# Attention: the high part of V's differences made on GpSimd, and scores emitted in parts of up to 512 keys

## The chip, the core and the metric

The kernel runs on one core of a Trainium2 chip. A core has TensorE (PE, matrix products; PEld is its loading of weights), VectorE (DVE), ScalarE (ACT) and GpSimd (POOL); SyncE (SP) issues the DMAs. Each engine works through its own instructions in order, and an instruction that waits holds up everything behind it on that engine. The metric is the device time of one execution in microseconds (us).

## The reference, cut to what matters

Two layers on a stream of 1024 positions of 1024 features: a Mamba-2 layer, then a layer of stick-breaking attention with 16 heads of 64 features. Between and after them stands a gated per-layer embedding. The change is in the attention:

```
for blk in range(s // SB_BLOCK):                       # 8 blocks of 128 queries
    z = einsum('bhtd,bhsd->bhts', q[:, :, q0:kend], k[:, :, :kend])
    log_keep = where(strict, log_sigmoid(-z), 0.0)
    suffix = cumsum(log_keep, reverse) - log_keep
    weights = where(strict, exp(log_sigmoid(z) + suffix), 0.0)
    outs.append(einsum('bhts,bhsd->bhtd', weights, v[:, :, :kend]))
```

With keep = sigmoid(-z), the product P of the keeps after a key is a running product, and a weight is a difference of two neighbouring P. So the kernel computes the running product P alone and multiplies it by the differences of neighbouring rows of V, which gives the same sum.

## The kernel before, in words

Matrix products of full precision are made from three products of two parts: a high part in the format that TensorE multiplies fast (`F32R`), and a low part, the value less its high part. The positions are stored in reverse, so that the keys of a query block come after it.

The attention takes two heads at a time, in 8 pairs (`hp`), and for each pair four steps p = 3, 2, 1, 0 of two query blocks: 32 steps, and two more to drain. Three things go on at once in `step(i)`:

- for step i itself, the projections of its two blocks (`project`, 24 products of 128x384 each, in four portions of six) and, for p = 3 and 2, half of the gate (`gate`, 24 products of 128x512). These are the filling: nothing in the same step needs them;
- for step i-1, `flip` (four transposes of the normalised k and q on TensorE, L879, then ACT and DVE write the high and low parts `kst`, `qh`, `ql`) and `scores` of two heads times two blocks: the products z (L901, L902), the sigmoid on ACT into `pt` (L903), and one running product (scan) on DVE along all keys of the block (L904);
- for step i-2, `turn` (transposes of `pt` on TensorE into `tr`, L916 and L919, the high part `wh` on ACT, L925, the low part `wl` on DVE, L926) and `product` with V (L936).

TensorE's order is written out by hand: a `manual_schedule` covers that engine alone. The pieces of steps i-1 and i-2 have positions between 0 and 1 (`SPREAD`, `FLIP`), and a piece comes when so much of the filling has been emitted. For p = 1 and 0 the filling counts 10 and its portions only add up to 8; for p = 3 and 2 it counts 17, and they add up to 14. The pieces with a position beyond 0.8 therefore stand at the end of a step with no filling between them. The order on ACT, DVE, POOL and SP is set by the scheduler.

At the end of step i, `values` makes the differences of V's rows: DMAs on SP copy `vr` one row on into `vs` (L847 is the large one), POOL subtracts (L853), ACT writes the high part into `V` (L858), and POOL writes the low part (L859). `vs` has one buffer; `V` has six, and its first reader is the product two steps later. `norm` then normalises k and q on DVE (L867 to L870). The PSUM tiles `tr` and `z` have two buffers each. The weights of the next pair are loaded and split into `g0h` (ACT, L104) and `g0l` (DVE, L108) along the way.

Of the kernel before, what the change touches and what calls it, by code (L numbers as in the profile page):

```python
# [8 lines left out]
F32 = mybir.dt.float32  # L9
# [4 lines left out]
ALU = mybir.AluOpType  # L14
# [4 lines left out]
P = 128  # L19
S = 1024  # L20
# [13 lines left out]
NEX = 5  # L34
EARLY = 3
LASTP = ((0, 0, 512), (1, 0, 256), (1, 256, 256))
SPREAD = ((0.05, 0.95), (0.7, 1.0))
FLIP = 0.55
FILL = {32: (7, (4, 5, 6, 7)), 33: (6, ())}
CHUNKS = {30: (0, 1, 2, 3)}  # L40

# [742 lines left out]
def attention(k, A, rawp, hT, oTd, dbg, b2, pairs):  # L784


    tc, nc = k.tc, k.nc
# [3 lines left out]
    with ExitStack() as ctx:  # L791
        pp = ctx.enter_context(tc.tile_pool(name="b_pair", bufs=1, reuse_waits="tile"))
        wk = ctx.enter_context(tc.tile_pool(name="b_work", bufs=2, reuse_waits="tile"))
# [6 lines left out]
        keep = pp.tile([P, S], BF16, name="keep")  # L800
# [7 lines left out]
        def begin_pair(st):  # L808
            st["V"], st["vr"], st["v0"] = {}, {}, {}
            st["GT"] = pairs.gt.tile([P, S], F32, name="GT")  # L810

        def project(st, b):
            W = st["W"]
            ps = mm.tile([P, 512], F32, name="mm")
            prs = []
            sl = slice(b % 4 * P, b % 4 * P + P)
            for kk in range(KT):
                whi, wlo = W[kk]
                prs += terms((hh[b // 4][:, kk, sl], hl[b // 4][:, kk, sl]), (whi[:, :384], wlo[:, :384]))
            yield from split3_some(nc, ps[:, :384], prs, 6)  # L820
            p = b // 2
            if b % 2:
                st["kq"] = wk.tile([P, 2, 2, P], F32, name="kq", bufs=2)
                st["vr"][p] = wk.tile([P, 2, P], F32, name="vr", bufs=3)
            nc.scalar.copy(st["kq"][:, b % 2], ps.rearrange("p (m c) -> p m c", c=256)[:, :, 0:128])
            nc.vector.tensor_copy(st["vr"][p][:, b % 2], ps[:, 128:256])  # L826
            yield

        def gate(st, half):
            W = st["W"]  # L830
            gp = mm.tile([P, 512], F32, name="mm")
            sl = slice(half * 512, half * 512 + 512)
            prs = []
            for kk in range(KT):
                whi, wlo = W[kk]
                prs += terms((whi[:, 384:], wlo[:, 384:]), (hh[half][:, kk], hl[half][:, kk]))
            yield from split3_some(nc, gp, prs, 4)
            sg = wk.tile([P, 512], F32, name="sg", bufs=1)
            nc.scalar.activation(sg, gp, AF.Sigmoid)
            nc.vector.tensor_tensor(st["GT"][:, sl], gp, sg, op=ALU.mult)  # L840
            yield

        def values(st, p):

            vr = st["vr"][p]
            vs = wk.tile([P, 2, P], F32, name="vs", bufs=1)
            nc.sync.dma_start(vs[0:P - 1], vr[1:P])  # L847
            nc.sync.dma_start(vs[P - 1:P, 0], vr[0:1, 1])
            nc.sync.dma_start(vs[P - 1:P, 1], st["vr"][p + 1][0:1, 0] if p < 3 else zrow)
            st["v0"][p] = sm.tile([P, 2], F32, name="v0", bufs=4)  # L850
            for i in range(2):
                nc.sync.dma_start(st["v0"][p][:, i:i + 1], vr[0:1, i])
            nc.gpsimd.tensor_tensor(vs, vs, vr, op=ALU.subtract)  # L853
            V = st["V"][p] = wk.tile([P, 2, 256], F32R, name="V", bufs=6)
            Vx = V.rearrange("p b (x c) -> p b x c", c=64)
            d = vs.rearrange("p b (h c) -> p b h c", c=64)
            for i in range(2):
                nc.scalar.copy(Vx[:, i, 0::3], d[:, i])  # L858
                nc.gpsimd.tensor_tensor(Vx[:, i, 1:3], d[:, i], Vx[:, i, 0::3].bitcast(F32), op=ALU.subtract)  # L859

        def norm(st, p):
# [11 lines left out]
        def flip(st, p):  # L873
            kn = st.pop(("kn", p))
            tsl = slice(p * 256, (p + 1) * 256)
            tq = trp.tile([P, 512], F32, name="tr")
            for i in range(2):
                for m in range(2):
                    nc.tensor.transpose(tq[:, m * 256 + i * P:m * 256 + (i + 1) * P], kn[:, i, m], ident)  # L879
            kt, qt = tq[:, 0:256], tq[:, 256:512]  # L880
            qh = wk.tile([P, 2, 256], F32R, name="qh", bufs=1)
            for h in range(2):
                o, x = own[h], own[1 - h]
                g = k.gkq[o]
                nc.scalar.activation(kst[o, h, tsl], kt[o], AF.Copy, scale=g)
                nc.vector.scalar_tensor_tensor(  # L886
                    kst[x, h, tsl], kt[o], g, kst[o, h, tsl].bitcast(F32), op0=ALU.mult, op1=ALU.subtract)
                nc.scalar.copy(qh[o, h], qt[o])
                nc.scalar.copy(qh[x, h], qt[o])
                nc.vector.tensor_tensor(ql[o, h], qt[o], qh[o, h].bitcast(F32), op=ALU.subtract)  # L890
            st["q", p] = qh

        def scores(st, h, b):
            qh = st["q", b // 2]
            N = (NT - b) * P
            qs = slice((b % 2) * P, (b % 2) * P + P)
            pt = wk.tile([P, S], F32, name="pt", bufs=5)
            for ko, n in ([(0, N)] if N <= 512 else [(0, N // 2), (N // 2, N // 2)]):
                z = zp.tile([P, 512], F32, name="z")
                rk = kst[:, h, b * P + ko:b * P + ko + n]  # L900
                nc.tensor.matmul(z[:, :n], lhsT=qh[:, h, qs], rhs=rk, start=True, stop=False)  # L901
                nc.tensor.matmul(z[:, :n], lhsT=ql[:, h, qs], rhs=rk, start=False, stop=True)  # L902
                nc.scalar.activation(pt[:, ko:ko + n], z[:, :n], AF.Sigmoid, scale=-1.0)  # L903
            nc.vector.tensor_tensor_scan(pt[:, :N], pt[:, :N], keep[:, :N], 1.0, op0=ALU.mult, op1=ALU.max)  # L904
            st["a", h, b] = pt

        def turn(st, p, h, j0):

# [57 lines left out]
        n = len(steps)  # L966

        def spread(fns, a, z):
            m = len(fns)
            return [(a + (z - a) * (i + 0.5) / m, f) for i, f in enumerate(fns)]  # L970

        def combine_pieces(st, p):

            units = [(h, j) for h in range(2) for j in range(2 * p, NT, 2)]
            def prod(h, j):
                product(st, p, h, j)
                if j == NT - 2:
                    fold(st, p, h)
            fns = []
            for i, (h, j) in enumerate(units):  # L980
                fns.append(lambda h=h, j=j: turn(st, p, h, j))
                if i >= 2:
                    fns.append(lambda u=units[i - 2]: prod(*u))
            return fns + [lambda u=u: prod(*u) for u in units[-2:]]

        def step(i):
            pieces = []
            if i >= 2:
                hp, p = steps[i - 2]
                pieces += spread(combine_pieces(sts[hp], p), *SPREAD[0])  # L990
            if 1 <= i <= n:
                hp, p = steps[i - 1]
                st = sts[hp]
                pieces.append((FLIP, lambda st=st, p=p: flip(st, p)))
                units = [(lambda st=st, h=h, b=b: scores(st, h, b)) for h in range(2) for b in (2 * p + 1, 2 * p)]
                pieces += spread(units, *SPREAD[1])
            pieces.sort(key=lambda x: x[0])
            fill = []
            if i < n:
                hp, p = steps[i]  # L1000
                if p == NT // 2 - 1:
                    pairs.all(hp)
                    begin_pair(sts[hp])
                    if hp + 1 < 8:
                        pairs.start(hp + 1)
                    else:
                        b2.begin(pairs)
                fill = [(project(sts[hp], 2 * p + 1), 5)]
                if p >= 2:
                    fill.append((gate(sts[hp], p - 2), 7))  # L1010
                fill.append((project(sts[hp], 2 * p), 5))
            total = sum(w for _, w in fill)
            done = 0
            for f, w in fill:
                for _ in f:
                    done += 1
                    while pieces and pieces[0][0] <= done / total:
                        pieces.pop(0)[1]()
            if i < n:
                if p in LOADS:  # L1020
                    pairs.step(hp + 1)
                values(sts[hp], p)
                norm(sts[hp], p)
                if i in CHUNKS:
                    b2.weights(CHUNKS[i])
            for _, f in pieces:
                f()
# [226 lines left out]
```

## Time and profile before

| what | value |
|---|---|
| median of 3 runs | 1968.86 us (1968.41 to 1986.42) |
| the profiled execution | 1967.15 us, of which the span is 1965.4 us |
| PE busy | 1757.7 us (89%) |
| DVE busy | 1174.0 us (60%) |
| ACT busy | 901.1 us (46%) |
| POOL busy | 377.3 us (19%) |
| chain that ended last | PE 59%, DMA 15%, DVE 15%, ACT 7% |
| the DMA from `vr` to `vs` in that chain | 13% |

The span runs from the first to the last instruction, and the rest of the execution's time lies around it. The chain that ended last is followed back from the last instruction, at each step to what released it. The attention takes from about 943 to about 1780 us of the span.

### The profile page before, as it was taken

Reading aid. Unit: us, or ns where it says so; the run is one execution under the profiler, and the core shown is the slowest. Engines: PE = TensorE matmul, PEld = TensorE weight load, DVE = VectorE, ACT = ScalarE, POOL = GpSimd, SP = SyncE. Lnnn points to the kernel's source line nnn. Section 1 sums busy time; section 2 is a strip of 40 time slices with the busy share of each in tenths; the row PEclk is TensorE's granted clock in tenths of the full one; section 3 lists DMA queues with packets and bytes.
Section 4 is the critical chain, followed back from the end, with each engine's and each line's share of the span. In section 5 each row is a group of like instructions: output and inputs, shape, how many; then the busy total and the mean of one; then the engine's idle time right before and its main releaser. Section 6 shows DMA issues by size and latency. Waiting matters only on the chain.

```text
span 1965.4 us, 25312 instructions
## 1 busy us (share of the span) xinstructions
PE 1757.7 (89%) x9170; PEld 1478.8 (75%) x9170; DVE 1174.0 (60%) x2462; ACT 901.1 (46%) x1974; POOL 377.3 (19%) x384
## 2 busy tenths in 40 slices
PE   7999999999999999999878787878788887679999
PEld 6778878878867878888877777777777776557887
DVE  6685484494596543456476767676767666754332
ACT  5566375375473321244363535454545443542121
POOL 0245445345342222000000000000000001111110
PEclk9999999999999999999989898989898998789999
DMA  4222222232136543222010101010101011223110
GB/s 145 72 81 97 70 86 82 70 91 92 58 94 202 171 144 118 88 87 97 9 58 18 47 18 48 18 47 18 48 18 48 17 38 49 70 86 98 58 49 32
DMA packets 96396, 139.41 MB, mean 71 GB/s; under 512 B 18160, under 2 KB 66640, under 8 KB 96272
## 3 DMA queue, kind: packets, MB, share of 16 engines
q1 hardware_dynamic: 96272, 137.80, 22.0%
q8 instruction: 72, 1.18, 0.2%
q14 instruction: 52, 0.43, 0.1%
HBM read 108.77 MB, written 24.77 MB: 68 GB/s over the span
## 4 chain that ended last, share of the span: by engine, by line
PE 59%; DMA 15%; DVE 15%; ACT 7%; issue 2%; POOL 2%; POOLq 0%; SPq 0%; DVEq 0%; ACTq 0%
PE mm L46 38%; DMA vs<-vr 13%; PE mm L53 8%; DVE pt L904 2%; PE pq L46 2%; DVE v L234 2%; PE intra L409 2%; DVE g0l L108 2%; DVE wl L926 2%; PE oq L936 1%; POOL vs L853 1%; PE inter L404 1%; PE tr L916 1%; PE tr L664 1%; DVE kst L886 1%
## 5 line engine op out<-in xcount | busy, mean ns | idle before, releaser
L46 PE MATMUL mm<-ul,wh 128*128 128x512 f32 (+1 forms) x648 | 254.0, 392 | 0.0
L46 PE MATMUL mm<-uh,wh 128*128 128x512 f32 (+1 forms) x648 | 252.6, 390 | 0.8 <-ACT v L232 0.7
L46 PE MATMUL mm<-uh,wl 128*128 128x512 f32 (+1 forms) x648 | 252.6, 390 | 0.0
L904 DVE TENSOR_TENSOR_SCAN pt<-pt,keep 128x128 f32<-128x128 f32 (+7 forms) x128 | 176.3, 1380 | 58.5 <-ACT pt L903 58.1
L53 PE MATMUL mm<-g0h,hh 128*128 128x384 f32 x512 | 188.5, 368 | 0.7 <-DVE vr L826 0.7
L53 PE MATMUL mm<-g0h,hl 128*128 128x384 f32 x512 | 176.4, 345 | 0.0
L53 PE MATMUL mm<-g0l,hh 128*128 128x384 f32 x512 | 176.2, 344 | 0.0
L926 DVE TENSOR_TENSOR wl<-tr,wh 128x512 fp32r<-128x512 f32 (+1 forms) x160 | 101.4, 634 | 120.5 <-ACT wh L925 118.0
L234 DVE SCALAR_TENSOR_TENSOR v<-u,convh,v 128x512 f32<-128x512 f32 x144 | 129.4, 903 | 53.5 <-ACT v L232 51.0
L853 POOL TENSOR_TENSOR vs<-vs,vr 128x256 f32<-128x256 f32 x32 | 23.3, 727 | 682.9 <-DMA vs<-vr 646.0
L916 PE MATMUL tr<-ident,pt 128*128 128x128 f32 x320 | 76.9, 288 | 81.5 <-DVE wl L926 79.5
L46 PEld LDWEIGHTS mm<-uh,wh 128*128 128x128 f32 x648 | 121.7, 188 | 27.0 <-ACT v L232 1.5
L46 PEld LDWEIGHTS mm<-ul,wh 128*128 128x128 f32 x648 | 121.7, 188 | 26.2 <-issue 2.3
L46 PEld LDWEIGHTS mm<-uh,wl 128*128 128x128 f32 x648 | 121.8, 188 | 25.8 <-issue 1.9
L925 ACT CAST wh<-tr 128x512 fp32r<-128x512 f32 (+1 forms) x160 | 85.0, 543 | 119.3 <-PE tr L919 118.2
L106 POOL TENSOR_TENSOR wl<-raw,wh 128x1024 fp32r<-128x1024 f32 x39 | 95.2, 2441 | 157.4 <-ACT wh L104 150.8
L901 PE MATMUL z<-kst,qh 128*128 128x320 f32 (+3 forms) x192 | 75.5, 393 | 52.4 <-ACT pt L903 44.0
L916 PEld LDWEIGHTS tr<-ident,pt 128*128 128x128 f32 x320 | 45.4, 145 | 93.4 <-DVE wl L926 86.3
L858 ACT CAST V<-vs 128x128 fp32r<-128x128 f32 x64 | 15.9, 295 | 197.5 <-POOL vs L853 197.5
L53 PEld LDWEIGHTS mm<-g0h,hh 128*128 128x128 f32 x512 | 100.3, 196 | 1.7 <-DVE vr L826 1.0
L53 PEld LDWEIGHTS mm<-g0l,hh 128*128 128x128 f32 x512 | 100.4, 196 | 0.7
L53 PEld LDWEIGHTS mm<-g0h,hl 128*128 128x128 f32 x512 | 99.3, 194 | 0.0
(350 smaller groups left out, 4376.3 us busy)
## 6 DMA issues: line engine op xcount, KB each, us to landing
raw<-in_w_in SPq DMA_DIRECT2D x40, 512.0 KB
ex<-acd SPq DMA_DIRECT2D x64, 256.0 KB
raw<-in_w_b SPq DMA_DIRECT2D x32, 512.0 KB
raw<-in_m_out SPq DMA_DIRECT2D x16, 512.0 KB
raw<-in_gate SPq DMA_DIRECT2D x16, 512.0 KB
graw<-gT SPq DMA_DIRECT2D x30, 256.0 KB
gT<-zs SPq DMA_DIRECT2D x28, 256.0 KB
acc<-in_x SPq DMA_DIRECT2D x8, 512.0 KB
```

Of the source, the lines that this page charges most:

```text
L46: nc.tensor.matmul(out, lhsT=a, rhs=b, start=(i == 0), stop=(i == n - 1))
L53: nc.tensor.matmul(out, lhsT=a, rhs=b, start=(i == 0), stop=(i == n - 1))
L106: (eng or nc.gpsimd).tensor_tensor(lo, raw, hi.bitcast(F32), op=ALU.subtract)
L108: nc.vector.scalar_tensor_tensor(lo, raw, gain, hi.bitcast(F32), op0=ALU.mult, op1=ALU.subtract)
L234: nc.vector.scalar_tensor_tensor(vv, u[:, 3 - j:3 - j + 512], w(j), vv, op0=ALU.mult, op1=ALU.add)
L409: nc.tensor.matmul(aq[hp * 64:hp * 64 + 64, jp * 256 + i * P:jp * 256 + (i + 1) * P], lhsT=xdts[2 * qt + i][:, (2 * j + hp) * 64:(2 * j + ...
L853: nc.gpsimd.tensor_tensor(vs, vs, vr, op=ALU.subtract)
L901: nc.tensor.matmul(z[:, :n], lhsT=qh[:, h, qs], rhs=rk, start=True, stop=False)
L904: nc.vector.tensor_tensor_scan(pt[:, :N], pt[:, :N], keep[:, :N], 1.0, op0=ALU.mult, op1=ALU.max)
L916: nc.tensor.transpose(tq[:, c:c + P], al[:, i0:i0 + P], ident)
L925: nc.scalar.copy(wh[:, :c], tq[:, :c])
L926: nc.vector.tensor_tensor(wl[:, :c], tq[:, :c], wh[:, :c].bitcast(F32), op=ALU.subtract)
```

## The change

The high part of V's differences is written by POOL in place of ACT, between POOL's two subtractions. `scores` gives out its parts singly, where before the two parts of a block with more than 512 keys came together; the scan follows the last part as before. The flip comes at position 0.5 of the filling in place of 0.55, and the scores are spread from 0.62 in place of 0.7.

```
-SPREAD = ((0.05, 0.95), (0.7, 1.0))
-FLIP = 0.55
+SPREAD = ((0.05, 0.95), (0.62, 1.0))
+FLIP = 0.5
...
             for i in range(2):
-                nc.scalar.copy(Vx[:, i, 0::3], d[:, i])
+                nc.gpsimd.tensor_copy(Vx[:, i, 0::3], d[:, i])
                 nc.gpsimd.tensor_tensor(Vx[:, i, 1:3], d[:, i], Vx[:, i, 0::3].bitcast(F32), op=ALU.subtract)
...
         def scores(st, h, b):
-            qh = st["q", b // 2]
             N = (NT - b) * P
             qs = slice((b % 2) * P, (b % 2) * P + P)
-            pt = wk.tile([P, S], F32, name="pt", bufs=5)
-            for ko, n in ([(0, N)] if N <= 512 else [(0, N // 2), (N // 2, N // 2)]):
+            parts = [(0, N)] if N <= 512 else [(0, N // 2), (N // 2, N // 2)]
+            def part(i):
+                qh = st["q", b // 2]
+                if i == 0:
+                    st["a", h, b] = wk.tile([P, S], F32, name="pt", bufs=5)
+                pt = st["a", h, b]
+                ko, n = parts[i]
                 z = zp.tile([P, 512], F32, name="z")
                 rk = kst[:, h, b * P + ko:b * P + ko + n]
                 nc.tensor.matmul(z[:, :n], lhsT=qh[:, h, qs], rhs=rk, start=True, stop=False)
                 nc.tensor.matmul(z[:, :n], lhsT=ql[:, h, qs], rhs=rk, start=False, stop=True)
                 nc.scalar.activation(pt[:, ko:ko + n], z[:, :n], AF.Sigmoid, scale=-1.0)
-            nc.vector.tensor_tensor_scan(pt[:, :N], pt[:, :N], keep[:, :N], 1.0, op0=ALU.mult, op1=ALU.max)
-            st["a", h, b] = pt
+                if i == len(parts) - 1:
+                    nc.vector.tensor_tensor_scan(pt[:, :N], pt[:, :N], keep[:, :N], 1.0, op0=ALU.mult, op1=ALU.max)
+            return [lambda i=i: part(i) for i in range(len(parts))]
...
-                units = [(lambda st=st, h=h, b=b: scores(st, h, b)) for h in range(2) for b in (2 * p + 1, 2 * p)]
+                units = [f for h in range(2) for b in (2 * p + 1, 2 * p) for f in scores(st, h, b)]
```

The first place is ACT's order at the end of a step p = 0, where the sigmoids of blocks 3 and 2 (640 and 768 keys, in halves of 320 and 384) are made. Before:

```order
L903 ACTIVATE pt<-z 128x384 x2
L104 ACTIVATE g0h<-raw,kvn 128x256
L104 ACTIVATE g0h<-raw,sn 128x256
L903 ACTIVATE pt<-z 128x320
L858 CAST V<-vs 128x2x64 x2
L903 ACTIVATE pt<-z 128x320
L947 COPY of<-oq 64x256
L903 ACTIVATE pt<-z 128x384 x2
```

The same place with the change (its lines are up to six numbers higher):

```order
L908 ACTIVATE pt<-z 128x384
L908 ACTIVATE pt<-z 128x320
L104 ACTIVATE g0h<-raw,kvn 128x256
L908 ACTIVATE pt<-z 128x320
L953 COPY of<-oq 64x256
L104 ACTIVATE g0h<-raw,sn 128x256
L908 ACTIVATE pt<-z 128x384 x2
```

The two casts into `V` are gone from between the sigmoids; on POOL they now stand between the subtraction L853 and the two subtractions L859 of the same step. Nothing else of ACT's work is added or removed.

The second place is TensorE in the same step, from the first score product on (`z` are scores, `oq` products with V, `mm` filling). Before:

```order
L901 MATMUL z<-kst,qh 128x320
L902 MATMUL z<-kst,ql 128x320
L901 MATMUL z<-kst,qh 128x320
L902 MATMUL z<-kst,ql 128x320
L936 MATMUL oq<-wh,V 128x256
L936 MATMUL oq<-wh,V 128x128
L936 MATMUL oq<-wl,V 128x256
L936 MATMUL oq<-wl,V 128x128
L901 MATMUL z<-kst,qh 128x384
L902 MATMUL z<-kst,ql 128x384
L901 MATMUL z<-kst,qh 128x384
L902 MATMUL z<-kst,ql 128x384
```

With the change:

```order
L906 MATMUL z<-kst,qh 128x320
L907 MATMUL z<-kst,ql 128x320
L942 MATMUL oq<-wh,V 128x256 x2
L942 MATMUL oq<-wl,V 128x256 x2
L906 MATMUL z<-kst,qh 128x320
L907 MATMUL z<-kst,ql 128x320
L53 MATMUL mm<-g0h,hh_6970 128x384
L53 MATMUL mm<-g0l,hh_6970 128x384
L53 MATMUL mm<-g0h,hl_6972 128x384
L53 MATMUL mm<-g0h,hh_6970 128x384
L53 MATMUL mm<-g0l,hh_6970 128x384
L53 MATMUL mm<-g0h,hl_6972 128x384
```

Before, all score products of this step came after its last filling. Now the first block's two parts stand apart, and a portion of filling comes after them; the later parts still follow with no filling between them.

## Rows read from the trace of the kernel before

**Rows 1.** Windows: length, busy us (instructions) of PE, PEld, DVE, ACT, POOL; PE clock; DMA.
```profile
1301.70:1400.70 99.00, 79.86 (x456) 72.36 (x456) 65.92 (x150) 47.70 (x115) 6.35 (x12) 0.91 0.11 33
```

**Rows 2.** One line's instructions, L858: count, min/median/max ns, first and last start.
```profile
L858 ACT CAST V<-vs x64: 292/295/298, 952.0 to 1708.4; 128x128 fp32r<-128x128 f32 x64
```

**Rows 3.** Waits from 950 to 1730 us: total us, times, longest.
```profile
PE tr L916 <- DVE wl L926: 78.8, 19, 6.8
PE z L901 <- ACT pt L903: 44.0, 31, 4.8
...
PE tr L879 <- DVE kq L870: 9.6, 2, 5.8
...
ACT V L858 <- POOL vs L853: 197.5, 32, 8.7
```

**Rows 4.** Chain that ended last, in order of time: start, us, what.
```profile
1323.43 2.02 DVE pt L904
1325.80 7.92 DMA vs<-vr
1333.88 0.73 POOL vs L853
...
1336.14 2.29 DVE pt L904
```

**Rows 5.** Timeline of PE, one pair of heads: start, us, idle before in brackets.
```profile
1302.56 0.69 PE L901 MATMUL z<-kst,qh 128*128 128x384 f32 x1 [4.35 <-ACT pt L903]
1339.34 0.47 PE L916 MATMUL tr<-ident,pt 128*128 128x128 f32 x1 [6.13 <-DVE wl L926]
1367.70 0.65 PE L879 MATMUL tr<-ident,kq 128*128 128x128 f32 x4 [2.05 <-DVE wl L926]
1382.40 0.44 PE L916 MATMUL tr<-ident,pt 128*128 128x128 f32 x2 [2.75 <-DVE wl L926]
```

**Rows 6.** Windows: four stretches that make up 99 us.
```profile
1283.38:1309.38 26.00, 18.91 (x99) 17.02 (x99) 21.16 (x52) 16.58 (x41) 1.59 (x3) 0.80 0.22 66
1309.38:1339.34 29.96, 23.62 (x140) 21.12 (x139) 19.12 (x35) 12.72 (x29) 1.58 (x3) 0.95 0.08 22
1339.34:1367.70 28.36, 26.31 (x157) 24.43 (x158) 15.37 (x42) 10.76 (x26) 1.59 (x3) 0.93 0.02 6
1367.70:1382.40 14.70, 10.98 (x63) 9.76 (x63) 10.27 (x26) 7.65 (x20) 1.59 (x3) 1.00 0.13 45
```

**Rows 7.** Windows: shorter stretches, for the granted clock.
```profile
1283.38:1294.00 10.62, 9.02 (x55) 7.93 (x55) 10.13 (x25) 9.28 (x23) 0.00 (x0) 1.00 0.32 99
1294.90:1305.60 10.70, 6.11 (x19) 5.38 (x20) 6.39 (x14) 5.27 (x14) 1.59 (x3) 0.52 0.05 12
...
1339.34:1345.00 5.66, 5.66 (x23) 4.92 (x24) 2.44 (x7) 1.03 (x2) 0.00 (x0) 0.66 0.01 0
```

**Rows 8.** Groups of POOL's instructions by form, whole span: count, busy us, mean ns.
```profile
L859 POOL TENSOR_TENSOR V<-vs,V 128x128 fp32r<-128x128 f32 x64 | 27.7, 454 | 12.6 <-ACT V L858 12.6
...
L802 POOL CAST keep<-tri 128x128 bf16<-128x128 f32 x1 | 0.3, 290 | 0.0
```

**Rows 9.** Timeline of POOL and DVE: two equal scans, one beside POOL's subtractions.
```profile
1302.05 0.86 POOL L859 TENSOR_TENSOR V<-vs,V 128x128 fp32r<-128x128 f32 x2 [0.41 <-ACT V L858]
...
1302.54 1.72 DVE L904 TENSOR_TENSOR_SCAN pt<-pt,keep 128x640 f32<-128x640 f32 x1 [4.19 <-ACT pt L903]
...
1392.00 1.49 DVE L904 TENSOR_TENSOR_SCAN pt<-pt,keep 128x640 f32<-128x640 f32 x1 [0.23 <-ACT pt L903]
```

**Rows 10.** Timeline of PE: a flip and the first score after it.
```profile
1286.31 0.60 PE L879 MATMUL tr<-ident,kq 128*128 128x128 f32 x4
...
1290.09 0.41 PE L901 MATMUL z<-kst,qh 128*128 128x320 f32 x1 [0.20 <-ACT qh L889]
```

**Rows 11.** Timeline of PE: a flip that waited for `norm`, and the last long wait.
```profile
969.93 0.63 PE L879 MATMUL tr<-ident,kq 128*128 128x128 f32 x4 [3.84 <-DVE kq L870]
...
1709.73 0.47 PE L916 MATMUL tr<-ident,pt 128*128 128x128 f32 x1 [6.77 <-DVE wl L926]
```

## The prediction

> **What bounds the kernel now.** I read the windows first. In the attention the time repeats every 99.0 us, once for each pair of heads, and of these 99.0 TensorE is busy for 79.86, DVE for 65.92, ACT for 47.70 [rows 1]. So TensorE stands idle for 19.1 us a pair although no engine is full: the stage is bound by waits. The view of waits says which. TensorE waited 78.8 us for `wl`, which DVE makes, and 44.0 us for `pt`, which ACT makes, 122.8 in all; and ACT itself waited 197.5 us in 32 times, once per step, before its cast into V [rows 3]. A pair has four such casts, and the 32 steps lie between 952.0 and 1708.4 us [rows 2].
>
> The chain of waits ties the two together. DVE ends a scan, the DMA from `vr` to `vs` takes 7.92 us, POOL subtracts for 0.73 us, and only then does ACT go on to the sigmoid and DVE to the next scan, of 2.29 us [rows 4]. That sigmoid needs nothing of V. It stands behind the cast in ACT's queue, the cast waits for the DMA, DVE waits for the sigmoid, and TensorE for DVE. The timeline of TensorE shows it four times a pair: 4.35, 6.13, 2.05 and 2.75 us [rows 5], 15.3 of the 19.1 us.
>
> TensorE also loses clock. Right after the 6.13 us wait it works for 5.66 us without a gap at a mean granted clock of 0.66; from 1294.9 to 1305.6 us, around the 4.35 us wait, it is busy for 6.11 us at 0.52, near the lower of its two levels of 1.2 and 2.4 GHz. But a stretch that began with a wait of that 2.75 us kind ran at 1.00 [rows 7]. So short waits can pass without a loss, long ones did not.
>
> **The change, part by part.** *The cast leaves ACT.* ACT's queue then holds nothing that waits for the DMA. What takes the place of each wait is worked out for the four stretches of a pair [rows 6].
>
> - 26.00 us, from 1283.38: DVE is busy for 21.16 of them and TensorE for 18.91, part of that at the lower clock. Without the 4.35 us wait DVE is the fuller engine, with the splitting of weights, four scans and `norm` in one queue. It cannot be shorter than DVE's 21.2; I take 21.5. Gain 4.5, clock included.
> - 29.96 us: TensorE 23.62, DVE 19.12. Four scans stand here, two of 2.02 and two of 2.29 us [rows 4]. From 1323.43 they alone reach 1332.1, the small DVE work between them some 2 us further, and `wl` comes after that, near 1334.7. TensorE had stopped at 1339.34 - 6.13 = 1333.2. So about 1.5 us of the 6.13 stay, less what the earlier scores bring; I take 1.1. Gain 5.0.
> - 28.36 us: the wait of 2.05 goes, and the 5.66 us at 0.66 become 5.66 x 0.66 = 3.7, 1.9 less. I keep 0.1 back. Gain 3.8.
> - 14.70 us: the 2.75 go. DVE's 10.27 leave room for it. Gain 2.75.
>
> Together 16.1 us a pair.
>
> *The cast goes to POOL.* POOL writes 64 pieces of 128x128. No row shows this cast on POOL with this output; the nearest are its cast of 128x128 to bf16, 290 ns, and its two-input subtraction of the same size, 454 ns [rows 8]. So 0.6 to 0.9 us a step, 19 to 29 us in all; I take 0.37 us each, between the two. V is ready some 0.5 us later than now, which costs nothing: its reader is a product two steps on, and the shortest step is over 10 us. The next step's DMA into the single `vs` buffer waits for POOL, but the loop (some 2 us of issuing, 7.92, then about 2.5 of POOL) is below 13 us a step, and a pair needs 4 x 13 = 52 of its 80.
>
> *POOL beside DVE.* Until now POOL's first subtraction fell into the time when all stood still. Now DVE works beside it. One row shows the price: a scan of 640 keys took 1.49 us alone and 1.72 when it started 0.37 us before POOL's subtractions ended (1302.05 + 0.86 against 1302.54) [rows 9]: 0.23 lost of 0.37. POOL will be busy for 0.73 + 2 x 0.37 + 0.86 = 2.3 us a step. Bounds: 0, and 2.3 x 0.62 = 1.4 us a step on the path. I take 0.3, since DVE is the limit in one stretch of four and half of its work has one operand in PSUM: 1.2 us a pair. The Trainium skill (SBUF — State Buffer, "Who interferes with whom") speaks against the move more strongly: a DVE instruction with two SBUF inputs and a POOL instruction that reads SBUF exclude each other, and whoever comes second waits for the first to end. By it the whole 0.37 us would have been lost.
>
> *Scores in parts, earlier.* The same matmuls and sigmoids, no instruction more. In a step p = 0 a portion of filling now stands behind the first block's two parts, which takes pressure from the two `z` buffers; but the flip is a little nearer to its first score. In the row it took 1290.09 - 1286.31 = 3.78 us with 0.20 of waiting [rows 10], and the cover shrinks by the 0.4 us of a product that moved behind the score; for p = 3 by about 1 us. Bounds: 1.5 us a pair gained, 2 lost; I take 0.5 lost.
>
> **The sum.** 16.1 - 1.2 - 0.5 = 14.4 us a pair, and 756 us [rows 2] hold 7.6 such periods: 109. The last long wait, 6.77 us [rows 11], lies in the drain, which the periods leave out; of it and the clock after it I take 5. So 114 us less than this execution's 1967.15, or 1853. The median of the runs is 1968.86, 1.7 above it. I predict 1852.
>
> **The rivals.**
>
> *DVE's queue takes over.* The waits on the scans stay twice as long as I think in the first two stretches, because DVE's 66 us a pair are bunched. Then 10 us a pair: 76 + 4, so 1887. For it: DVE is already the fuller engine for 26 of 99 us. Against it: 14 us a pair in which it waited for ACT become free.
>
> *POOL shuts DVE out.* All of POOL's 2.3 us a step delay DVE, and all of it on the path: 9.2 us a pair in place of 1.2. That leaves 6.4 a pair, 49 + 5: 1913. For it: the slower scan of [rows 9]. Against it: one scan in four stands there, and the rest of DVE's work has room in three stretches. It is the rule of the page named above taken to its end.
>
> *All waits go.* The 122.8 us of [rows 3] and the clock (1.9 and 6.11 x 0.48 = 2.9 a pair, 36 us) would give 1808; with the 1.1 us a pair kept, some 1816.
>
> *The wait only moves.* V is late for its product and TensorE waits for the same DMA there: 1965. Against it: two steps of room. A change that is not made as told can be excluded: the order of ACT shows the casts gone.
>
> *Slower: the flip waits for `norm`.* The flip comes earlier by one portion of filling, and its input is the last of `norm`'s eleven small DVE instructions. One flip did wait 3.84 us for them [rows 11]. If each of the 32 did, it would cost 123 us against 114 gained; from 3.6 us a flip on the kernel is slower, and at 5 us it takes 2012. Against it: only two flips of 32 did [rows 3], and DVE comes to `norm` sooner once it no longer waits for ACT.
>
> **Chances and range.** The forecast (1835 to 1870) 0.55; DVE's queue 0.17; POOL shuts DVE out 0.10; all waits go 0.13; the wait moves 0.03; slower 0.02. The range from 1822 to 1896 holds the forecast, DVE's queue and the half of "all waits go" that stops short: 0.8. A measurement of this kernel can tell about 1% from no change, 20 us. Faster by more than that 0.95, within it 0.03, slower 0.02.
>
> **What would show it.** In the changed profile ACT should have no wait for POOL's subtraction, and its wait of 197.5 us should be gone, not shared out. A pair should take about 84.6 us in place of 99.0, with TensorE's idle time at 6 to 9 us and a granted clock above 0.95. What is left of TensorE's waits should be for `wl` behind scans at the end of p = 3 and p = 0, with DVE busy up to them and no longer waiting for ACT. If TensorE waits for V, the fifth rival is right; if the scans grow by more than 0.5 us on average, POOL is what costs; if flips wait for `kq`, the last. I am wrong in the main step if ACT's wait is gone and a pair still takes over 90 us.

## The result and the profile after

The changed kernel takes 1833.58 us in the median of 4 runs (1832.00 to 1837.69). The kernel before, run beside it on the same chip, takes 1977.64 us (4 runs, 1968.41 to 1987.79). The ratio is 0.927 with an interval of [0.921, 0.934], so the kernel is 6.6 to 7.9% faster. The runs of the kernel before lie near 1967 and near 1987 us here and in eight of the twelve comparisons below, and that is what makes several intervals wide. The profiled execution takes 1837.69 us and its span is 1836.0; that is 129.4 us less span than before.

The page of the changed kernel, busy time and the chain that ended last:

```profile
PE 1725.0 (94%) x9170; PEld 1452.7 (79%) x9170; DVE 1189.7 (65%) x2462; ACT 894.6 (49%) x1910; POOL 402.2 (22%) x448
...
PE 67%; DVE 20%; ACT 7%; DMA 3%; issue 2%; POOL 0%; SPq 0%; DVEq 0%; ACTq 0%
```

The DMAs' share of the chain fell from 15% to 3%, and TensorE is busy for 94% of the span in place of 89%.

Windows of the changed kernel: four pairs of heads, one after another, and the whole attention (columns as in [rows 1]):

```profile
1079.81:1161.21 81.40, 74.90 (x457) 68.47 (x456) 67.47 (x150) 46.73 (x106) 9.43 (x20) 1.00 0.12 40
1161.21:1243.01 81.80, 75.24 (x457) 68.56 (x456) 67.59 (x152) 46.75 (x106) 9.42 (x20) 1.00 0.13 40
1243.01:1327.45 84.44, 77.80 (x457) 70.78 (x456) 67.62 (x151) 46.73 (x106) 9.42 (x21) 0.96 0.12 38
1327.45:1410.56 83.11, 76.63 (x456) 69.95 (x456) 67.51 (x151) 46.73 (x106) 9.43 (x21) 0.98 0.13 39
943.00:1650.60 707.60, 630.94 (x3702) 569.78 (x3701) 568.61 (x1238) 394.16 (x879) 94.31 (x169) 0.97 0.16 49
```

The attention of the kernel before, in the same view; what follows it takes 185.4 us in both:

```profile
943.00:1780.00 837.00, 662.66 (x3695) 594.86 (x3694) 551.33 (x1235) 400.21 (x942) 68.78 (x105) 0.90 0.14 41
```

A pair now takes (1410.56 - 1079.81) / 4 = 82.7 us where it took 99.0 [rows 1], and TensorE is idle for 6.5 to 6.6 of them (81.40 - 74.90 in the first line) where it was for 19.1. The attention is shorter by 837.00 - 707.60 = 129.4 us, which is the whole difference of the spans. Of that, 97.7 us are TensorE's idle time (174.3 before, 76.7 after) and 31.7 us are its busy time, for the same matmuls: 662.66 against 630.94. That second part goes with the clock, 0.90 before and 0.97 after.

Waits of the changed kernel from 950 to 1650 us, TensorE and then ACT (total us, times, longest), against [rows 3]:

```profile
PE tr L922 <- DVE wl L932: 28.9, 22, 5.2
PE z L906 <- ACT pt L908: 15.8, 30, 1.1
PE z L906 <- ACT qh L889: 12.1, 9, 3.6
PE tr L879 <- DVE kq L870: 5.8, 2, 4.5
...
ACT wh L931 <- PE tr L925: 154.0, 101, 4.5
ACT kst L885 <- PE tr L879: 38.9, 23, 4.7
```

ACT's 197.5 us for POOL's subtraction are gone. ACT now waits longest for TensorE's transposes: it waits for the bound of the stage, no longer for the DMA into `vs`. Of TensorE's 122.8 us for `wl` and `pt`, 44.7 are left.

The chain of the changed kernel through one such place, against [rows 4] (start, us, what):

```profile
1178.05 2.20 DVE pt L910
1180.31 1.93 DVE pt L910
1182.33 0.44 DVE of L954
...
1182.96 2.19 DVE pt L910
1185.21 0.78 DVE GT L959
...
1186.99 0.57 DVE wl L932
```

There is no DMA between the scans any more. Here DVE is limited by its own queue: three scans of this step and the small work between them, and then the `wl` for which TensorE waits.

POOL's groups by form in the changed kernel, against [rows 8] (busy us, mean ns):

```profile
L859 POOL TENSOR_TENSOR V<-vs,V 128x128 fp32r<-128x128 f32 x64 | 32.1, 522 | 0.0
...
L858 POOL CAST V<-vs 128x128 fp32r<-128x128 f32 x64 | 20.3, 345 | 2.1
```

The cast takes 345 ns in the mean, between the bounds of 290 and 454. The subtractions behind it went from 454 to 522 ns, with DVE now at work beside them.

Scans of the changed kernel from 943 to 1570 us, by form:

```profile
L910 DVE TENSOR_TENSOR_SCAN pt<-pt,keep 128x640 f32<-128x640 f32 x14 | 20.8, 1488 | 0.3
...
L910 DVE TENSOR_TENSOR_SCAN pt<-pt,keep 128x128 f32<-128x128 f32 x16 | 8.5, 532 | 0.0
```

The same forms in the kernel before, from 943 to 1670 us:

```profile
L904 DVE TENSOR_TENSOR_SCAN pt<-pt,keep 128x640 f32<-128x640 f32 x14 | 22.3, 1590 | 26.6 <-ACT pt L903 26.6
...
L904 DVE TENSOR_TENSOR_SCAN pt<-pt,keep 128x128 f32<-128x128 f32 x16 | 6.7, 420 | 0.3
```

The 26.6 us of idle time in front of the scans of 640 keys are gone. Their mean fell by 0.10 us, because the one in each pair that ran beside POOL's subtractions [rows 9] now runs alone. The mean of the 128-key scans rose by 0.11 us through a single one of the 16, which met one of POOL's subtractions for weights of the next stage. The two in the timeline of the changed kernel:

```profile
1536.12 2.41 POOL L106 TENSOR_TENSOR hl<-raw,hh 128x1024 fp32r<-128x1024 f32 x1 [18.07 <-ACT hh L104]
...
1536.55 2.27 DVE L910 TENSOR_TENSOR_SCAN pt<-pt,keep 128x128 f32<-128x128 f32 x1
```

It took 2.27 us where the others take 0.42: 1.85 us were lost of the 1.98 for which POOL was still at work. The change itself costs the scans nothing: all 128 of them take 176.3 us before and 177.0 now. What grew is DVE's other work, among it `norm`'s small steps (L77 to L79, from 47.6 to 55.9 us) and the splits of `g0l` for two of the weights (from 60.9 to 65.2).

### The profile page after: what moved, and what is told of

Its sections match the earlier page's. It is cut to its first block, busy times and chain, and to the rows that moved or that the text cites. A ratio compares the mean times of both kernels' runs of the same rounds, so it can differ in the third digit from the quotient of the medians.

```text
span 1836.0 us, 25269 instructions
## 1 busy us (share of the span) xinstructions
PE 1725.0 (94%) x9170; PEld 1452.7 (79%) x9170; DVE 1189.7 (65%) x2462; ACT 894.6 (49%) x1910; POOL 402.2 (22%) x448
## 4 chain that ended last, share of the span: by engine, by line
PE 67%; DVE 20%; ACT 7%; DMA 3%; issue 2%; POOL 0%; SPq 0%; DVEq 0%; ACTq 0%
PE mm L46 40%; PE mm L53 12%; DVE pt L910 6%; PE pq L46 2%; PE oq L942 2%; DVE v L234 2%; PE intra L409 2%; DVE g0l L108 1%; PE tr L922 1%; DVE wl L932 1%; PE inter L404 1%; ACT pt L908 1%; PE tr L664 1%; DMA raw<-in_gate 1%; PE tr L925 1%
## 5 line engine op out<-in xcount | busy, mean ns | idle before, releaser
L53 PE MATMUL mm<-g0h,hh 128*128 128x384 f32 x512 | 182.7, 357 | 0.0
L910 DVE TENSOR_TENSOR_SCAN pt<-pt,keep 128x128 f32<-128x128 f32 (+7 forms) x128 | 177.0, 1386 | 0.8 <-ACT pt L908 0.3
L234 DVE SCALAR_TENSOR_TENSOR v<-u,convh,v 128x512 f32<-128x512 f32 x144 | 129.4, 904 | 53.5 <-ACT v L232 51.0
L853 POOL TENSOR_TENSOR vs<-vs,vr 128x256 f32<-128x256 f32 x32 | 24.1, 754 | 550.3 <-DMA vs<-vr 319.1
L932 DVE TENSOR_TENSOR wl<-tr,wh 128x512 fp32r<-128x512 f32 (+1 forms) x160 | 101.5, 635 | 43.8 <-ACT wh L931 41.6
L922 PE MATMUL tr<-ident,pt 128*128 128x128 f32 x320 | 75.4, 284 | 31.5 <-DVE wl L932 28.9
L574 DVE SCALAR_TENSOR_TENSOR acc<-mm,rg,acc 128x512 f32<-128x512 f32 x64 | 47.8, 749 | 84.9 <-PE mm L46 83.5
L53 PEld LDWEIGHTS mm<-g0h,hh 128*128 128x128 f32 x512 | 96.6, 189 | 1.0
L647 DVE SCALAR_TENSOR_TENSOR pth<-pth,pq 128x512 f32<-128x512 f32 (+1 forms) x33 | 22.2, 672 | 113.8 <-PE pq L46 109.1
```

The source lines that it names most:

```text
L53: nc.tensor.matmul(out, lhsT=a, rhs=b, start=(i == 0), stop=(i == n - 1))
L234: nc.vector.scalar_tensor_tensor(vv, u[:, 3 - j:3 - j + 512], w(j), vv, op0=ALU.mult, op1=ALU.add)
L574: nc.vector.scalar_tensor_tensor(acc[:, sl], ps, k.rg[:, g, t:t + 1], acc[:, sl], op0=ALU.mult, op1=ALU.add)
L922: nc.tensor.transpose(tq[:, c:c + P], al[:, i0:i0 + P], ident)
L932: nc.vector.tensor_tensor(wl[:, :c], tq[:, :c], wh[:, :c].bitcast(F32), op=ALU.subtract)
```

## The experiments

The theory: the cast in ACT's queue waited for the DMA and held up the sigmoids behind it, and taking this wait away is the gain. Against it stand three others: that the scores' parts and places bring it; that ACT was freed of work (or POOL does this work better), wait or not; and that DVE, or POOL's use of memory beside it, sets what is left.

**The cast alone, in the kernel before.**

```diff
-                nc.scalar.copy(Vx[:, i, 0::3], d[:, i])
+                nc.gpsimd.tensor_copy(Vx[:, i, 0::3], d[:, i])
```

> The kernel before, with the cast into V on POOL and nothing else changed. Theory A (ACT's queue stood still behind a cast that waits for the DMA, and that wait is nearly all of the gain): 1840 to 1860 us, ACT's wait for POOL's subtraction gone, a pair of heads at 83 to 86 us. Rival B (the parts of the scores and their earlier places carry the gain, the cast little): 1920 to 1965 us.

Measured: 1867.61 us (1864.34 to 1872.62, 4 runs) against 1968.49, ratio 0.947 [0.940, 0.954], some 8 us above what was expected. The cast alone brings 101 us. The places and parts bring the rest, 34 us down to 1833.58, which the prediction had not seen. Two stretches of a pair show what is left. Timeline of TensorE in this kernel, the end of a step p = 0 and the third turn of the next step (idle time before in brackets):

```profile
1157.66 0.44 PE L901 MATMUL z<-kst,qh 128*128 128x384 f32 x1 [0.79 <-ACT pt L903]
...
1159.93 0.64 PE L901 MATMUL z<-kst,qh 128*128 128x320 f32 x1 [0.91 <-ACT pt L903]
...
1196.34 0.47 PE L916 MATMUL tr<-ident,pt 128*128 128x128 f32 x1 [3.14 <-DVE wl L926]
```

Windows of the same kernel there, and four whole pairs:

```profile
1155.00:1160.00 5.00, 2.96 (x13) 2.05 (x13) 4.70 (x9) 4.82 (x13) 0.00 (x0) 0.80 0.66 204
1160.00:1165.00 5.00, 5.00 (x17) 4.67 (x18) 4.91 (x12) 3.89 (x10) 0.00 (x0) 0.51 0.08 22
...
1196.33:1202.50 6.17, 6.17 (x21) 5.29 (x22) 2.44 (x7) 0.58 (x1) 0.00 (x0) 0.51 0.02 0
...
1070.27:1414.92 344.65, 313.65 (x1825) 285.05 (x1825) 272.08 (x601) 186.81 (x425) 41.29 (x80) 0.96 0.13 37
```

The waits of 4.35 and 6.13 us [rows 5] have shrunk to 0.91 and 3.14, but the clock is still low at both places: 0.51 in each, where it was 0.52 and 0.66 [rows 7]. A pair takes 86.2 us in the mean of the four (84.8 to 87.6), of which TensorE is idle for 7.8.

**Parts and places alone, with the cast still on ACT.** The changed kernel, with

```diff
-                nc.gpsimd.tensor_copy(Vx[:, i, 0::3], d[:, i])
+                nc.scalar.copy(Vx[:, i, 0::3], d[:, i])
```

> The changed kernel with the cast into V back on ACT: only the scores' parts and the earlier places of flip and scores remain. Theory A: 1945 to 1970 us, ACT again waits some 150 to 200 us for POOL's subtraction, TensorE loses clock after it. Rival B: 1840 to 1880 us.

Measured: 1982.43 us (1979.52 to 1986.00, 10 runs), ratio 1.005 [1.001, 1.008]: nothing gained, at most a little lost, and slower than the 1970 us that were expected at most. ACT's waits in this kernel, 950 to 1730 us:

```profile
ACT V L858 <- POOL vs L853: 207.6, 32, 8.7
```

The wait is still there, 32 times. So the places bring their 34 us only once the cast is gone; the two parts of the change do not simply add.

**The cast on DVE.** The changed kernel, with

```diff
-                nc.gpsimd.tensor_copy(Vx[:, i, 0::3], d[:, i])
+                nc.vector.tensor_copy(Vx[:, i, 0::3], d[:, i])
```

> The changed kernel with the cast into V on DVE. DVE's queue then stands still behind the same DMA four times a pair, and TensorE waits for DVE's wl and ACT's flips. Theory A: 1930 to 2000 us, DVE waiting 150 us or more for POOL's subtraction. Rival C (any engine other than ACT will do, only load counts): 1835 to 1860 us.

Measured: 2036.18 us (2034.89 to 2037.07, 4 runs), ratio 1.032 [1.025, 1.038], still slower than expected. DVE's waits in this kernel, 950 to 1780 us:

```profile
DVE V L858 <- POOL vs L853: 150.1, 31, 6.0
```

And one of them in DVE's timeline, with the scan that stands behind it:

```profile
1233.43 0.36 DVE L858 CAST V<-vs 128x128 fp32r<-128x128 f32 x2 [4.84 <-POOL vs L853]
...
1234.61 1.74 DVE L910 TENSOR_TENSOR_SCAN pt<-pt,keep 128x768 f32<-128x768 f32 x1
```

ACT is as free of the cast here as in the changed kernel, and the time is 203 us worse (2036.18 against 1833.58). The same wait stands in front of the scans themselves. What counts is not that ACT is relieved but in whose queue the wait stands.

**The cast on ACT, one step later.** The changed kernel with the subtraction, the cast (on ACT) and the low part written out one step later:

```diff
-            nc.gpsimd.tensor_tensor(vs, vs, vr, op=ALU.subtract)
+            late.append((st, p, vs, vr))
+        late = []
+        def finish():
+            st, p, vs, vr = late.pop(0)
+            nc.gpsimd.tensor_tensor(vs, vs, vr, op=ALU.subtract)
...
-                nc.gpsimd.tensor_copy(Vx[:, i, 0::3], d[:, i])
+                nc.scalar.copy(Vx[:, i, 0::3], d[:, i])
...
+            if late:
+                finish()
             if i < n:
```

> The changed kernel with the cast on ACT, but the subtraction, the cast and the low part of a step are made at the end of the next step, when the DMA into vs has had a whole step to land. ACT has the same work as before the change, only nothing to wait for. Theory A (it was the wait in the queue): 1830 to 1855 us, ACT's wait for POOL's subtraction below 30 us in all. Rival C (ACT's 19 us of casts were what cost, or POOL must be free for V early): 1870 to 1970 us.

Measured: 1949.04 us (1947.57 to 1950.13, 4 runs), ratio 0.988 [0.982, 0.994]: a miss, and one that tells nothing of the theory. ACT's waits in this kernel, 950 to 1780 us:

```profile
ACT V L864 <- POOL vs L859: 201.5, 32, 8.7
```

The wait was not removed. The order on ACT is the scheduler's, and the cast still came upon an unfinished DMA. A version without the wait had to be made another way.

**The cast on ACT, with no DMA to wait for.** The changed kernel with the cast on ACT again, the same 64 pieces, but taken from `vr`, which DVE writes and from which the DMA starts, in place of the difference:

```diff
-                nc.gpsimd.tensor_copy(Vx[:, i, 0::3], d[:, i])
+                nc.scalar.copy(Vx[:, i, 0::3], vr[:, i].rearrange("p (h c) -> p h c", c=64))
```

> The changed kernel with the cast back on ACT, but reading vr in place of the difference in vs, so that it has nothing to wait for: it leaves out the shift and the subtraction in the high part. ACT has the same 64 casts as before the change; the DMA and POOL's subtractions are all there. Theory A (it was the wait in ACT's queue, not the 19 us of work): 1825 to 1845 us. Rival C (ACT's work costs): 1850 us or more.

Measured: 1831.39 us (1827.86 to 1833.59, 4 runs) against 1967.21, ratio 0.931 [0.929, 0.932], as fast as the changed kernel. The line's instructions in this kernel (min/median/max ns, first and last start), and what ended ACT's idle time before them (us, times):

```profile
L858 ACT CAST V<-vr x64: 282/298/309, 934.7 to 1568.5; 128x128 fp32r<-128x128 f32 x64
...
  DVE vr L826: 39.8, 25
```

ACT does the 64 casts at 298 ns, where it took 295 before [rows 2]. They still wait for DVE's `vr`, 39.8 us in 25 times, but not for the DMA, and the kernel loses nothing by them. This shows the cause: it was the wait for the DMA in front of the sigmoids, neither ACT's work nor a merit of POOL. It also shows what POOL's casts cost DVE: without them it is busy for 1189.5 us, with them for 1189.7.

**POOL's low part three times.** The changed kernel, with

```diff
+            for i in range(2):
+                for _ in range(2):
+                    nc.gpsimd.tensor_tensor(Vx[:, i, 1:3], d[:, i], Vx[:, i, 0::3].bitcast(F32), op=ALU.subtract)
```

> The changed kernel with the two low-part subtractions of each step made three times over, so that POOL reads SBUF beside DVE for 2 us a step longer, 66 us in all. If what POOL takes from DVE lies on the path as the prediction's bound has it (0.62 of each us): 1834 + 40 = 1874 us. If it hides in DVE's slack, as the forecast's 0.3 us a step for 2.3 us of POOL: 1834 + 9 = 1843 us. DVE's busy time should grow in either case.

Measured: 1837.45 us (1830.70 to 1839.54, 4 runs), ratio 0.934 [0.933, 0.936]. Busy time on the page of this kernel, against that of the changed kernel above:

```profile
PE 1721.1 (94%) x9170; PEld 1447.5 (79%) x9170; DVE 1200.1 (66%) x2462; ACT 894.4 (49%) x1910; POOL 465.2 (25%) x576
```

POOL works 63.0 us more (465.2 against 402.2), DVE's same 2462 instructions become longer by 10.4 us together (1200.1 against 1189.7), and the kernel's median by 3.9 us, with runs that overlap. So POOL's reads do slow DVE, and DVE's slack takes nearly all of it. The Trainium skill (SBUF — State Buffer, "Who interferes with whom") says that a DVE instruction with two inputs in SBUF and a POOL instruction that reads SBUF shut each other out. The rows agree: `norm`'s small steps, with two inputs in SBUF, went from 55.9 to 63.2 us and the two splits `g0l` from 65.2 to 69.7, while `wl`, with one input in PSUM, stayed at 101.5 and 101.4; the 128-key scan of 2.27 us above lost nearly all of the time for which POOL was still at work. How much of DVE's work POOL's longer work met was not measured. The rival in which all of POOL's work falls on the path is excluded.

**Single parts at the old places.** The changed kernel, with

```diff
-SPREAD = ((0.05, 0.95), (0.62, 1.0))
-FLIP = 0.5
+SPREAD = ((0.05, 0.95), (0.7, 1.0))
+FLIP = 0.55
```

> The changed kernel with flip and scores at their old places (0.55, 0.7), the parts single. The cast alone gave 1867.6 us and all of it 1833.6. If splitting the blocks into parts carries these 34 us: 1835 to 1845 us. If the earlier places carry them: 1855 to 1868 us.

Measured: 1869.11 us (1867.11 to 1871.15, 4 runs), ratio 0.950 [0.948, 0.951], which is the 1867.61 of the cast alone. Giving out the parts singly does nothing by itself.

**Whole blocks at the new places.** The changed kernel, with the parts of a block together again:

```diff
-            return [lambda i=i: part(i) for i in range(len(parts))]
+            return [lambda: [part(i) for i in range(len(parts))]]
```

> The changed kernel with the new places (0.5, 0.62) but a block's two parts together as before. If the earlier places carry the 34 us: 1833 to 1845 us. If the single parts carry them: 1855 to 1868 us.

Measured: 1829.38 us (1829.06 to 1830.41, 4 runs), ratio 0.930 [0.928, 0.931]. That is 4 us below the changed kernel, and each of its runs is faster than any of that kernel, but the two ratios do not tell them apart. So the places carry all of the 34 us.

**Whole blocks, the new place for the flip alone.** As the last, and

```diff
-SPREAD = ((0.05, 0.95), (0.62, 1.0))
+SPREAD = ((0.05, 0.95), (0.7, 1.0))
```

> Cast on POOL, whole blocks, the flip at 0.5, the scores from 0.7 as before. The places together gave 38 us over the kernel with the cast alone (1867.6 against 1829.4). If the scores' places carry them, by pulling the scans forward so that the third turn's transposes wait less for wl and the clock stays up: 1855 to 1868 us. If the flip's place carries them, by ending the wait of the first scores for qh and ql: 1829 to 1845 us.

Measured: 1858.66 us (1856.40 to 1858.88, 4 runs), ratio 0.941 [0.936, 0.947]. Taken in this order, the flip's place brings about 9 us (from 1867.61), the scores' place some 29 (to 1829.38); the scores' place without the flip's was not run. Windows of this kernel, the end of a step p = 0:

```profile
1150.00:1155.00 5.00, 3.12 (x22) 2.96 (x20) 4.54 (x12) 4.24 (x11) 0.00 (x0) 1.00 0.38 108
1155.00:1160.00 5.00, 4.28 (x16) 3.69 (x17) 4.65 (x7) 4.17 (x11) 0.00 (x0) 0.66 0.37 117
```

The clock still falls there. The same place in the changed kernel, and below it three stretches that begin with the third turn:

```profile
1229.00:1234.00 5.00, 3.79 (x22) 3.25 (x22) 4.55 (x9) 4.78 (x13) 0.00 (x0) 1.00 0.34 105
1234.00:1239.00 5.00, 4.18 (x24) 3.90 (x25) 4.91 (x9) 4.94 (x14) 0.00 (x0) 1.00 0.04 11
1187.61:1193.70 6.09, 6.09 (x36) 5.28 (x37) 3.47 (x10) 1.18 (x2) 0.00 (x0) 1.00 0.02 0
1269.25:1275.25 6.00, 6.00 (x21) 5.12 (x21) 2.77 (x9) 0.59 (x1) 0.00 (x0) 0.50 0.02 0
1353.71:1359.71 6.00, 6.00 (x27) 5.22 (x28) 3.12 (x10) 1.17 (x2) 0.00 (x0) 0.72 0.03 3
```

And TensorE's timeline in the changed kernel, the longest wait for a sigmoid at that place and two of the third turns:

```profile
1187.61 0.33 PE L922 MATMUL tr<-ident,pt 128*128 128x128 f32 x1 [2.72 <-DVE wl L932]
...
1234.48 0.41 PE L906 MATMUL z<-kst,qh 128*128 128x320 f32 x1 [1.09 <-ACT pt L908]
...
1269.25 0.47 PE L922 MATMUL tr<-ident,pt 128*128 128x128 f32 x1 [2.69 <-DVE wl L932]
```

With the new places filling stands among the scores of p = 0. Waits of 1.09 us are still there, no shorter than the 0.91 of the cast alone. But TensorE is busy for 3.79 and 4.18 of 5.00 us, and the clock stays at 1.00, where 2.96 of 5.00 were followed by 0.51. It is so pair by pair: in five in a row, the 15 us from the first score of such a step on run at 0.77 or 0.89 with the flip alone (with the cast alone in four of the five), and at 1.00 in all five in the changed kernel and with whole blocks at its places. So the gain of the places is in good part clock. Four pairs of the changed kernel, and four of the kernel with whole blocks at the same places:

```profile
1066.37:1397.13 330.76, 304.58 (x1825) 277.77 (x1825) 270.21 (x601) 186.94 (x425) 37.70 (x80) 0.98 0.12 39
1067.51:1394.92 327.41, 305.08 (x1825) 279.60 (x1825) 266.81 (x601) 184.96 (x425) 38.74 (x80) 0.98 0.12 39
```

Four pairs of the cast alone took 344.65 us with TensorE busy for 313.65. Of the 13.9 us less in the changed kernel 9.1 are busy time and 4.8 idle time; with whole blocks it is 8.6 and 8.7 of 17.2. Half to two thirds is clock, and the rest is shorter waits.

**Still earlier.** Three kernels: the changed one (single parts) and whole blocks with the flip at 0.4 and the scores from 0.5 to 0.84, so that no block, and of eight single parts only the last, is left at the end of a step without filling, and whole blocks with values in between:

```diff
-SPREAD = ((0.05, 0.95), (0.62, 1.0))
-FLIP = 0.5
+SPREAD = ((0.05, 0.95), (0.5, 0.84))
+FLIP = 0.4
```

> The changed kernel with flip at 0.4 and scores from 0.5 to 0.84, so that no score is left to the end of a step. If scores without filling between them are what still costs: 1815 to 1828 us. If DVE is the limit there, or the flip now waits for the normalised k and q: 1834 to 1860 us.

Measured: 1836.25 us (1834.71 to 1839.52, 4 runs) against 1968.57, ratio 0.930 [0.925, 0.936].

> As the last, with a block's two parts together. Same two cases: 1812 to 1826 us, or 1830 to 1860 us.

Measured: 1831.68 us (1830.15 to 1833.11, 4 runs), ratio 0.928 [0.921, 0.934]. Neither is better than the places of the change. TensorE's waits in the first of the two, 950 to 1570 us, say why:

```profile
PE tr L879 <- DVE wl L932: 19.6, 13, 1.7
PE tr L922 <- DVE wl L932: 13.9, 27, 0.9
```

The wait for `wl` did not shrink but moved in part to the flips, where the changed kernel has none of it; in the same stretch that kernel waits 22.9 us for `wl`, all in its turns. In the second kernel the flips wait 20.4 us in the same way. The expected case in which DVE is the limit came in.

The third has whole blocks and

```diff
-SPREAD = ((0.05, 0.95), (0.62, 1.0))
-FLIP = 0.5
+SPREAD = ((0.05, 0.95), (0.57, 1.0))
+FLIP = 0.45
```

> Cast on POOL, whole blocks, flip at 0.45, scores from 0.57 to 1.0: one place earlier in the steps p = 3 and 2, nearly the same in p = 1 and 0. If the wait for wl behind the scans in p = 3 is what is left (1.96 us a pair with whole blocks): 1815 to 1826 us. If not: 1827 to 1835 us.

Measured: 1823.46 us (1820.45 to 1823.79, 4 runs), ratio 0.923 [0.918, 0.929], the fastest of all, and faster in every run than the changed kernel in any, though the intervals of the two ratios overlap. Its timeline at the third turn, and a window over five pairs:

```profile
1182.94 0.33 PE L922 MATMUL tr<-ident,pt 128*128 128x128 f32 x1 [1.38 <-DVE wl L932]
```

```profile
1000.00:1400.00 400.00, 375.29 (x2291) 344.53 (x2290) 334.18 (x749) 232.04 (x531) 48.27 (x100) 1.00 0.13 42
```

The wait of 2.7 us has become 1.38 and the clock does not fall in 400 us. TensorE is busy for 94% of them.

## Why the prediction was right, and where its sizes were off

*The main step holds.* ACT's wait for the DMA was the cause. It is gone, not shared out, and the cast on ACT without that DMA in front of it gives the same time. A pair takes 82.7 us where 84.6 were forecast, and TensorE is idle for 6.5 where 6 to 9 were. In the pairs shown the clock is 0.96 to 1.00. What is left is most of all for `wl` behind scans, 28.9 us. The time, 1833.58, lies inside the range and 18 us below the forecast, just under its core of 1835 to 1870. That it lies so near is partly luck, since two errors have opposite signs: the cast's 118 us forecast and the places' 34 us measured would together have given 1817, below the range. Some 3 us of the 18 are a slip at the end of the sum, where 1853 and 1.7 make 1855 and not 1852.

*The cast was worth less than its terms.* They gave (16.1 - 1.2) x 7.6 + 5 = 118 us; the cast alone brought 101, and 12.8 us a pair (99.0 to 86.2) in place of 14.9. Two terms failed. "Gain 4.5, clock included" took the low clock at the end of p = 0 to follow from the 4.35 us wait; with the wait gone the clock was at 0.51 all the same. And of the 6.13 us, 3.14 stayed where 1.1 were forecast: DVE's queue between the scans was longer than the 2 us allowed for it (from the first scan at 1183.41 to `wl` at 1195.72 it is 12.3 us, of which the four scans take 8.4), and behind this wait the clock was 0.51 as well. This is a part of the rival in which DVE's queue takes over, in one place of a pair, not in two.

*The scores' places were mis-sized, with the wrong sign.* Forecast: 0.5 us a pair lost, 4 in all, with a bound of 1.5 a pair gained. Measured: 34 us gained, 3.5 a pair (86.2 against 82.7). The prediction priced the waits that the order changes and not the clock, though it had read the low clock at just that place in [rows 7]. The part that it named as the change, single parts, does nothing; the part that it mentioned in passing, the places, does all.

*POOL was priced about right, by a wrong share.* The cast takes 345 ns where 370 were taken. DVE's work grew from 65.92 to some 67.5 us a pair, 1.6, of which little lies on the path: 63.0 us more of POOL's work cost 3.9. The bound of 1.4 us a step on the path did not come near. Its 0.62, from 0.23 us lost of 0.37, is not a share that holds: scans lost 1.85 of 1.98 us here, 1.43 of 1.56 (the 768 keys at 1572.57) and, in the kernel before, 1.78 of 1.92 (the 256 keys at 1654.53), each time 0.13 to 0.14 us less than POOL still needed. The price stayed small because in the pairs the scans hardly meet POOL. And of DVE's 65.9 us a pair 27 have an operand in PSUM, less than the half that was taken.

*The slower rival did not come.* Flips waited for `kq` twice, 5.8 us in all, as seldom as before [rows 3]. A slower kernel from a moved wait does exist, but by another way: the cast on DVE takes 2036.

## What to carry to other kernels

Look in each engine's queue for an instruction that waits for a DMA and has nothing to do with the work behind it; it costs what the whole chain behind it loses, and it belongs on an engine that has nothing urgent behind it. Moving it onto the next busy engine can make things worse. When the waits are gone, look at the granted clock stretch by stretch: a few portions of filling among products that wait were worth a third of what the wait itself was (34 and 101 us), half to two thirds of it through the clock.

## What the runs showed of the hardware

The clock did not follow from the length of a wait alone. Third turns that waited 2.72 and 2.69 us were followed by some 6 us at 1.00 and at 0.50, near the upper and the lower of the two levels of 2.4 and 1.2 GHz, in one execution of one program. The Trainium skill (TensorE: Matmul & The Clock Gate, "What's actually happening") says that the clock follows how busy the engine has been of late, and that the point at which it changes varies with when the work falls; these rows agree. Nor is a long wait needed: with the cast alone the clock fell to 0.51 where no wait was longer than 0.91 us and TensorE was busy for 2.96 of the 5.00 us in which it fell.

POOL's reads beside DVE were almost free for the kernel, 3.9 us for 63.0 us of POOL's work, because DVE had slack; for DVE itself they were not, at 10.4 us. A scan that started beside a two-input subtraction of POOL lost the time that POOL still needed less 0.13 to 0.14 us, in the four cases given, from 0.37 to 1.98 us.
